# More turns between a triangular solve and its product, and two small stores issued from ScalarE, in a hybrid decoder layer

## The chip, the cores and the metric

The kernel runs on one core of a Trainium2 chip. Its engines are TensorE (PE), VectorE (DVE), ScalarE (ACT), GpSimd (POOL) and SyncE (SP, which only issues transfers here). The metric is the device time of one execution in microseconds. A core has 16 DMA engines; transfers are issued from the queues of SP, ACT and POOL.

## What is computed

One inference step of one decoder layer for a prompt of 512 tokens and for 8 single sample tokens, with the same weights. Cut to what matters:

```python
def layer(x, c, buf_k, buf_v, S0, shift0):
    mod = jax.nn.silu(c) @ w_ada + b_ada
    sh1, sc1, gt1, sh2, sc2, gt2 = jnp.split(mod, 6, axis=-1)
    h = _modulate(_rmsnorm(x, g_norm_mix), sh1, sc1)
    q, k, v, p_rwkv = jnp.split(h @ w_in, ATTN_SPLITS, axis=-1)
    # samples: k_all = the 128 cached rows and the new row; likewise v_all
    att = _banded_attention(q, k_all, v_all, q_pos, k_pos, attn_sinks)
    new_k, new_v = k_all[:, T:], v_all[:, T:]       # the last 128 rows
    rw, S, last_row = _rwkv7_mix(p_rwkv, shift0, S0, ...)
    x = x + gt1[:, None, :] * (jnp.concatenate([att, rw], axis=-1) @ w_out)
    h2 = _modulate(_rmsnorm(x, g_norm_ffn), sh2, sc2)
    gate, up = jnp.split(h2 @ w_ffn_in, 2, axis=-1)
    x = x + gt2[:, None, :] * ((jax.nn.silu(gate) * up) @ w_ffn_out)
    return x, new_k, new_v, S, last_row
# inside _rwkv7_mix, per head, token after token:
#   S_t = S_{t-1} diag(w_t) + (S_{t-1} a_t) b_t^T + v_t k_t^T ;  y_t = S_t r_t
```

Everything is float32. The model has width 2048, 16 query heads and 4 key heads of 64 in the attention half, 16 heads of 64 in the RWKV half.

## The kernel before

**Stages.** The start computes the modulation and the norm. Then comes the RWKV stage, in which the columns of `w_in` are multiplied tile by tile, and the recurrence of the 16 heads runs beside it, two heads (a pair) at a time, eight pairs. Next are the attention beside the first parts of `w_out`, the rest of `w_out`, the first FFN product and the second.

**Products.** A float32 product is made of three float32r products of high and low halves. `unit` loads 128x512 weights from SP's queue (`raw`, three buffers), ScalarE casts the high half (`wh`), VectorE subtracts for the low half (`wl`), and `mm3` issues one *group*: six matmuls of 128x260, the pairs of `wh` and high, `wh` and low, `wl` and high. One unit serves four groups.

**Turns.** After each group the main loop calls `pump`, which gives a turn to each background job that is due. Jobs are Python generators: what one does up to its next `yield` is written into the program at that place. So a bare `yield` in a loop lets more main groups be written ahead of the job's next step. Paced engine wrappers add estimated costs, from which a job's next due time comes. The framework then orders each engine's instructions from what was written, with ready work ahead of waiting work, so one moved step moves its neighbours too. Each engine works through its own order strictly from the front; only its waits are on other engines.

**The solve.** The recurrence is done in chunks of 32 tokens. Per pair, `rwkv_rest` solves 32x32 triangular systems on VectorE (`Tt`, 31 steps of two instructions). The result is written to DRAM (`TTd`, four transfers, two from SP and two from POOL) and read back in another layout (`Td`, from POOL). VectorE copies it into block-diagonal form (`TT`). Then come a number of bare turns, and then for each of the two heads the product `pu` of `L3` and `TT` on PE. After that the chain over the 16 chunks begins (`psc` on PE, `Z` on ScalarE), four small matmuls a turn. The jobs of several pairs are under way at the same time: `rwkv_prep1` and `rwkv_prep2` prepare the next pair (`pw`, `pa`, `pn`, `pG`, `pA`, `pT`, `pg`, `pb`; `lf` are their small weights). `ada_gen` multiplies the rest of the modulation weights (`ada`, weights `ar`). None of them depends on `w_in`'s main tiles except through the buffers.

**The new rows.** At the attention's start `kv_gen` loads keys and values, transposes the values, and `new_kv_sample` transposes the samples' new key and value rows (`KVS`) into `ptx`. VectorE copies them to `kst`, a buffer of the tag `q` (four buffers), and to `VSt`. Two transfers of 8 KB write them to the outputs `ks` and `vs`. The tag `q` is used in turn by the two value loads, `kst`, and the query tiles of `attn_pair`, so the fourth query tile takes `kst`'s place:

```python
q = ap.tile([P, T], F32, tag="q", bufs=4, name=self.nm("q"))
nc.sync.dma_start(q, self.qd[t])
```

Other loads of that time: `x1` (520 KB each) and `s3`, weights of the FFN loaded ahead from SP and added to from POOL (`accum_op`, L1503 and L1504). `attn_decode` computes the samples' attention with the small products `plx` and `psc`. PSUM tiles of `aux` have two buffers, used in turn by all jobs; `plx` takes one that the products `pl` of `attn_pair` held, which VectorE reads with a mask row (`Lg`, `sm`).

Of the kernel before, what the change touches and what calls it, by code (L numbers as in the profile page):

```python
# [63 lines left out]
class Kern:  # L64
# [642 lines left out]
    def rwkv_rest(self, d):  # L707
        nc, I, rc = self.px, self.I, self.rc
        hp, L3, PC = (d[n] for n in ("hp", "L3", "PC"))
# [25 lines left out]
        for c4 in range(4):  # L735
            ro = slice(32 * c4, 32 * c4 + 32)
            nc.vector.tensor_copy(TT[ro, :, 32 * c4:32 * c4 + 32], Td[ro])
        for _ in range(8):
            yield
        for e in range(2):  # L740
            pu = self.aux("pu")
# [143 lines left out]
    def new_kv_sample(self):  # L885
        nc, I, O, ap = self.px, self.I, self.O, self.ap
        pt = self.aux("ptx")
        for i in range(4):
            nc.tensor.transpose(pt[0:8, i * 128:(i + 1) * 128], self.KVS[:, i].rearrange("p h s -> p (h s)"), self.ident)
        kt = ap.tile([8, 256], F32, tag="q", bufs=4, name="kst")  # L890
        self.VSt = ap.tile([8, 256], F32, name="VSt")
        nc.vector.tensor_copy(kt, pt[0:8, 0:256])
        nc.vector.tensor_copy(self.VSt, pt[0:8, 256:512])
        nc.gpsimd.dma_start(O["ks"][:, 127, :], kt)
        nc.gpsimd.dma_start(O["vs"][:, 127, :], self.VSt)

    def attn_pair(self, t, d):
        nc, I, ap = self.px, self.I, self.ap
# [856 lines left out]
```

## Time and profile before

| | |
|---|---|
| median of 3 runs | 2631.68 us (2631.5 to 2631.95) |
| the profiled execution | 2632.03 us, its span 2630.3 us |
| PE busy | 2526.8 us (96%) |
| VectorE busy | 1650.7 us (63%) |
| ScalarE busy | 1167.3 us (44%) |
| POOL busy | 382.3 us (15%) |
| granted PE clock, mean | 0.98 |
| moved by DMA | 460.20 MB, mean 175 GB/s |

A row of the timeline reads: start, duration, engine, line, operation, tile written, tile read, shapes, count; in brackets the idle time of the engine ahead of it and what ended that. Matmuls overlap, so their durations are longer than the time from start to start. A row of the windows reads: stretch, its length, then busy time and count of PE, weight loads, VectorE, ScalarE and POOL, and at the end the granted PE clock, the share of the DMA engines and the GB/s. A row of the waits reads: who waited for whom, total us, times, longest. Instructions issued through the pacing wrapper all have the line L49, so tiles tell them apart. SPq, ACTq and POOLq are transfers being issued.

### The profile page before, as it was taken

The numbers are of one execution on the slowest core, as the hardware profiler recorded it, in microseconds if no ns is written. First come the engines' busy times: TensorE is split into PE (matmuls) and PEld (weight loads), VectorE is DVE, ScalarE is ACT, GpSimd is POOL, SyncE is SP. The second block draws the span as 40 slices with busy tenths as digits, with TensorE's granted clock in tenths as the row PEclk, the third lists the DMA queues.
The fourth block names the chain that finished last, engine by engine and source line by source line (L and its number), as shares of the span: only waits on it lengthen the run. The fifth ranks groups of instructions, "written<-read, shape, count | busy, mean of one in ns | idle before, by whom it ended". The sixth has DMA issues, their size and how long they took to land. (4 is left out here: it accounts for less than half of the span.)

```text
span 2630.3 us, 58954 instructions
## 1 busy us (share of the span) xinstructions
PE 2526.8 (96%) x23373; PEld 2359.7 (90%) x23373; DVE 1650.7 (63%) x3628; ACT 1167.3 (44%) x2413; POOL 382.3 (15%) x529
## 2 busy tenths in 40 slices
PE   7898999999999999998999999999999999999998
PEld 4587878887888988898999999999999999999997
DVE  5566554766656453678777777777777763444456
ACT  3233556566545333557444444444444432222225
POOL 0011111221203010021122122122122000000003
PEclk9998999999999997999999999999999999999999
DMA  9865556655433674246587687688688353443333
GB/s 341 297 202 182 164 172 220 193 189 172 140 111 129 216 224 120 93 156 204 156 228 210 170 218 213 168 214 222 164 214 224 114 181 93 125 126 102 116 105 110
DMA packets 241797, 460.20 MB, mean 175 GB/s; under 512 B 32480, under 2 KB 44656, under 8 KB 241488
## 3 DMA queue, kind: packets, MB, share of 16 engines
q1 hardware_dynamic: 206320, 377.25, 43.8%
q0 software_dynamic: 34560, 78.13, 13.5%
q8 instruction: 183, 3.00, 0.5%
q10 hardware_dynamic: 640, 1.05, 0.2%
q14 instruction: 94, 0.77, 0.1%
HBM read 421.73 MB, written 35.59 MB: 174 GB/s over the span
## 5 line engine op out<-in xcount | busy, mean ns | idle before, releaser
L89 ACT CAST wh<-raw 128x512 fp32r<-128x512 f32 (+2 forms) x410 | 247.4, 606 | 474.2 <-PE pf L99 286.0
L92 DVE TENSOR_TENSOR wl<-raw,wh 128x512 fp32r<-128x512 f32 (+2 forms) x410 | 285.1, 698 | 244.9 <-ACT wh L89 238.5
L99 PE MATMUL pf<-go,wh 128*128 128x260 f32 x2560 | 414.1, 281 | 0.0
L99 PEld LDWEIGHTS pf<-go,wh 128*128 128x128 f32 x2560 | 354.0, 188 | 0.1
L1283 ACT CAST wh<-sr 128x512 fp32r<-128x512 f32 x320 | 197.9, 621 | 258.0 <-PE pm L1454 223.8
L99 PE MATMUL pm<-hH,wh 128*128 128x260 f32 (+1 forms) x1248 | 291.1, 313 | 7.2 <-ACT wh L89 6.4
L1284 DVE TENSOR_TENSOR wl<-sr,wh 128x512 fp32r<-128x512 f32 x320 | 220.2, 688 | 83.1 <-ACT wh L1283 76.0
L99 PE MATMUL pf<-go,wl 128*128 128x260 f32 x1280 | 267.7, 282 | 0.0
L99 PE MATMUL pm<-hH,wl 128*128 128x260 f32 (+1 forms) x1248 | 262.8, 290 | 5.0 <-DVE wl L92 4.9
L1454 PE MATMUL pm<-xT,wh 128*128 128x260 f32 x1408 | 263.1, 286 | 1.1 <-DVE pc L1531 0.6
L99 PE MATMUL pm<-hL,wh 128*128 128x260 f32 (+1 forms) x1248 | 259.3, 289 | 0.0
L1454 PE MATMUL pm<-T,wh 128*128 128x260 f32 x1408 | 257.6, 283 | 0.0
L99 PEld LDWEIGHTS pm<-hH,wh 128*128 128x128 f32 (+1 forms) x1248 | 194.3, 190 | 46.5 <-issue 19.7
L1454 PEld LDWEIGHTS pm<-xT,wh 128*128 128x128 f32 x1408 | 216.8, 188 | 7.7 <-DVE pc L1531 2.8
L1454 PEld LDWEIGHTS pm<-T,wh 128*128 128x128 f32 x1408 | 216.9, 188 | 0.0
L99 PEld LDWEIGHTS pm<-hH,wl 128*128 128x128 f32 (+1 forms) x1248 | 196.4, 191 | 13.8 <-DVE wl L92 8.3
L1454 PE MATMUL pm<-B0H,wl 128*128 128x260 f32 x704 | 200.9, 286 | 7.7 <-DVE wl L1284 7.1
L1454 PE MATMUL pm<-B0H,wh 128*128 128x260 f32 x704 | 200.1, 284 | 2.9 <-DVE acct L1220 1.6
L99 PEld LDWEIGHTS pf<-go,wl 128*128 128x128 f32 x1280 | 201.0, 188 | 0.0
L99 PEld LDWEIGHTS pm<-hL,wh 128*128 128x128 f32 (+1 forms) x1248 | 195.6, 191 | 4.5 <-issue 2.9
L1454 PE MATMUL pm<-T,wl 128*128 128x260 f32 x704 | 198.7, 282 | 0.3 <-DVE wl L1284 0.3
L1454 PE MATMUL pm<-B0L,wh 128*128 128x260 f32 x704 | 198.9, 283 | 0.0
(425 smaller groups left out, 5236.8 us busy)
## 6 DMA issues: line engine op xcount, KB each, us to landing
ar<-in_w_ada SPq DMA_DIRECT2D x256, 256.0 KB, 4.2
sr<-in_w_fi SPq DMA_DIRECT2D x176, 256.0 KB, 4.4
raw<-in_w_fo SPq DMA_DIRECT2D x176, 256.0 KB, 2.6
raw<-in_w_in SPq DMA_DIRECT2D x144, 256.0 KB, 3.9
araw<-in_w_ada SPq DMA_DIRECT2D x64, 512.0 KB, 6.6
raw<-in_w_fi SPq DMA_DIRECT2D x120, 256.0 KB, 4.3
s<-in_w_fi SPq DMA_DIRECT2D x80, 256.0 KB, 5.9
s<-in_w_fi POOLq DMA_DIRECT2D x80, 256.0 KB, 7.2
```

The costliest lines, as they stand in the source:

```text
L89: nc.scalar.copy(wh[:, :n], raw[:, :n])
L92: nc.vector.tensor_tensor(wl[:, :n], raw[:, :n], wh[:, :n].bitcast(F32), ALU.subtract)
L99: nc.tensor.matmul(ps[:m, bank, :HB], w, a[:, k, h, :], start=first and i == 0, stop=last and i == 2, skip_group_check=True,)
L1283: nc.scalar.copy(H, src)
L1284: nc.vector.tensor_tensor(L, src, H.bitcast(F32), ALU.subtract)
L1454: nc.tensor.matmul(ps[:, :HB], x[:, s], y, start=g == k == i == 0, stop=g == 1 and k == 3 and i == 2, skip_group_check=True)
```

## The change

`rwkv_rest` takes 18 bare turns instead of 8 between the copy into `TT` and the product for the first pair (`hp` 0), and 10 instead of 8 for the seven others. `new_kv_sample` issues its two stores from ScalarE's queue instead of POOL's.

```diff
@@ rwkv_rest
         for c4 in range(4):
             ro = slice(32 * c4, 32 * c4 + 32)
             nc.vector.tensor_copy(TT[ro, :, 32 * c4:32 * c4 + 32], Td[ro])
-        for _ in range(8):
+        for _ in range(18 if hp == 0 else 10):
             yield
         for e in range(2):
             pu = self.aux("pu")
@@ new_kv_sample
         nc.vector.tensor_copy(kt, pt[0:8, 0:256])
         nc.vector.tensor_copy(self.VSt, pt[0:8, 256:512])
-        nc.gpsimd.dma_start(O["ks"][:, 127, :], kt)
-        nc.gpsimd.dma_start(O["vs"][:, 127, :], self.VSt)
+        nc.scalar.dma_start(O["ks"][:, 127, :], kt)
+        nc.scalar.dma_start(O["vs"][:, 127, :], self.VSt)
```

In the order of the instructions these places change. The rows are in the order in which the engine takes them; a row reads: line, operation, tile written, tiles read, shape, count. `pm` is the main product of `w_in`, and the numbers tell buffers apart. On PE, ahead of the first pair's first `pu`, before:

```order
L99 MATMUL pm_2994<-hH,wl_2998 128x260 x2
L322 MATMUL ada_2861<-ar_2963,cT 32x128 x4
L322 MATMUL ada_2861<-ar_2964,cT 32x128
L49 MATMUL pu_2983<-TT,L_288_1790 128x128 x4
L322 MATMUL ada_2861<-ar_2964,cT 32x128 x3
```

and after:

```order
L99 MATMUL pm_2988<-hH,wl_3082 128x260 x2
L322 MATMUL ada_2861<-ar_3051,cT 32x128 x4
L322 MATMUL ada_2861<-ar_3052,cT 32x128 x4
L322 MATMUL ada_2861<-ar_3053,cT 32x128 x4
L322 MATMUL ada_2861<-ar_3054,cT 32x128 x4
L49 MATMUL pu_3113<-TT,L_288_1790 128x128 x4
```

The product stands behind later weight units and a later round of `ada`. On VectorE, at the copy into `TT` of the same pair, before:

```order
L92 TENSOR_TENSOR wl_3088<-raw_3085,wh_3087 128x512
L49 SCALAR_TENSOR_TENSOR tF_2657<-pc_2167,par,tF_2657 128x512
L49 COPY TT<-Td_2828 32x8x32 x4
L49 SCALAR_TENSOR_TENSOR tA_2780<-tF_2657,tA_2780 128x512
L92 TENSOR_TENSOR lf_3134<-raw_3135,lf_3134 128x256
```

and after:

```order
L49 SCALAR_TENSOR_TENSOR tF_2657<-pc_2167,par,tF_2657 128x512
L92 TENSOR_TENSOR lf_3124<-raw_3125,lf_3124 128x256
L49 COPY TT<-Td_2828 32x8x32 x4
L49 SCALAR_TENSOR_TENSOR tA_2780<-tF_2657,tA_2780 128x512
L92 TENSOR_TENSOR wl_3082<-raw_3079,wh_3081 128x512
```

The cut of `lf` has moved ahead of the copy, and a cut of a main weight unit follows it. On POOL, at the attention's start:

```order
 L49 DMA out_vp<-Vt 128x256
 L1504 DMA s_2308_16277<-in_w_fi 128x512
-L49 DMA out_ks<-kst 8x256
-L49 DMA out_vs<-VSt 8x256
 L1504 DMA s_2333_16418<-in_w_fi 128x512
 L1504 DMA s_2352_16546<-in_w_fi 128x512
```

The two stores leave POOL's queue; on ScalarE they come between two casts of `w_out` weights. In PE's order nothing is moved from the attention's start on.

## The prediction

> **What bounds the kernel now.** I read the page first, then the chain of waits, PE's list of waits, and the timelines around the two places that the diff touches.
>
> ```profile
> span 2630.3 us, 58954 instructions
> 2116.30 477.88 PE pf L99 x3984
> PE pu L49 <- DVE TT L49: 18.4, 5, 10.1
> PE plx L49 <- DVE sm L49: 5.5, 1, 5.5
> PE po L99 <- ACT wh L89: 3.3, 1, 3.3
> PE ssq L402 <- DVE tC L400: 10.4, 3, 10.0
> ```
>
> The second row is from the chain of waits: at the end PE runs 478 us without a gap, and the chain ahead of it is PE again. So time that PE loses anywhere earlier is lost at the end, one for one. Of PE's waits, the first row of the four is exactly the product `pu` that the change moves; the second is in the attention decode, and it will turn out to hang on the two stores.
>
> **The first pair's product.** PE, then VectorE, POOL and SyncE around it:
>
> ```profile
> 247.69 0.40 PE L99 MATMUL pm<-hH,wh 128*128 128x260 f32 x2
> 247.93 0.40 PE L99 MATMUL pm<-hL,wh 128*128 128x260 f32 x2
> 248.16 0.40 PE L99 MATMUL pm<-hH,wl 128*128 128x260 f32 x2
> 248.49 0.62 PE L322 MATMUL ada<-ar,cT 128*32 128x128 f32 x10
> 259.17 2.04 PE L49 MATMUL pu<-TT,L 128*128 128x128 f32 x8 [10.05 <-DVE TT L49]
> 266.55 1.08 PE L322 MATMUL ada<-ar,cT 128*32 128x128 f32 x32
> 247.87 0.17 DVE L724 TENSOR_TENSOR Tt<-Tt,stmp 128x8 f32<-128x8 f32 x1
> 257.84 1.18 DVE L49 COPY TT<-Td 32x256 f32<-32x256 f32 x4 [4.85 <-DMA Td<-TTd]
> 259.05 0.69 DVE L49 SCALAR_TENSOR_TENSOR tA<-tF,tA 128x512 f32<-128x512 f32 x1
> 251.73 0.92 POOL L732 DMA_DIRECT2D Td<-TTd  x1 [2.21 <-DMA TTd<-Tt]
> 250.20 1.81 SPq L317 DMA_DIRECT2D ar<-in_w_ada  x4
> ```
>
> The solve ends at 248.04, its result goes out to DRAM and back, lands at 257.84, and VectorE has copied it by 259.02. PE was there at 249.11 and waits 10.05 us. The change doesn't shorten that trip; it only puts more PE work ahead of the wait. One turn with work is one group of six matmuls, 3 x 0.24 = 0.72 us from start to start (first three rows). PE before and after, ahead of the first `pu`:
>
> ```order
> L99 MATMUL pm_2994<-hH,wh_2997 128x260 x2
> L99 MATMUL pm_2994<-hL,wh_2997 128x260 x2
> L99 MATMUL pm_2994<-hH,wl_2998 128x260 x2
> L322 MATMUL ada_2861<-ar_2963,cT 32x128 x4
> L322 MATMUL ada_2861<-ar_2964,cT 32x128
> L49 MATMUL pu_2983<-TT,L_288_1790 128x128 x4
> ```
>
> ```order
> L99 MATMUL pm_2988<-hH,wl_3042 128x260 x2
> L99 MATMUL pm_2988<-hH,wh_3081 128x260 x2
> L99 MATMUL pm_2988<-hL,wh_3081 128x260 x2
> L99 MATMUL pm_2988<-hH,wl_3082 128x260 x2
> L99 MATMUL pm_2988<-hH,wh_3081 128x260 x2
> L99 MATMUL pm_2988<-hL,wh_3081 128x260 x2
> L99 MATMUL pm_2988<-hH,wl_3082 128x260 x2
> L322 MATMUL ada_2861<-ar_3051,cT 32x128 x4
> L322 MATMUL ada_2861<-ar_3052,cT 32x128 x4
> L322 MATMUL ada_2861<-ar_3053,cT 32x128 x4
> L322 MATMUL ada_2861<-ar_3054,cT 32x128 x4
> L49 MATMUL pu_3113<-TT,L_288_1790 128x128 x4
> ```
>
> Counted over the whole order, `pu` now comes 9 groups and 27 `ada` matmuls later: 9 x 0.72 = 6.5, and 27/16 x 1.08 = 1.8 (the profile has two records for each `ada` matmul), together 8.3 us. But the third of the weight units now ahead of `pu` (3081, 3082) needs its low half from VectorE, and there it stands behind the copy that waits:
>
> ```order
> L92 TENSOR_TENSOR wl_3042<-raw_3039,wh_3041 128x512
> L49 SCALAR_TENSOR_TENSOR tF_2657<-pc_2167,par,tF_2657 128x512
> L92 TENSOR_TENSOR lf_3124<-raw_3125,lf_3124 128x256
> L49 COPY TT<-Td_2828 32x8x32 x4
> L49 SCALAR_TENSOR_TENSOR tA_2780<-tF_2657,tA_2780 128x512
> L92 TENSOR_TENSOR wl_3082<-raw_3079,wh_3081 128x512
> ```
>
> Before, the two units in front of `pu` were both cut ahead of the copy. So PE will wait again, for `wl` in place of `TT`: the copy ends at 259.02, the row at 259.05 takes 0.69, a cut 0.65, which makes 260.35. Then 0.24 + 0.72 + 1.08 of PE work are left, and `pu` starts at 262.4, 3.2 us later than before with 8.3 us more done. Gain 8.3 - 3.2 = **5.1 us**. The `ada` weights on the way (issued at 250.20) land near 255; that splits the wait in two and leaves its end where it is. What else is new ahead of the copy is the cut of `lf`, whose load takes the place in SyncE's queue that a load of twice its size had; it should land before Td. Bounds: 0 (the copy comes 5 us later) to 8.3.
>
> The pause also costs clock:
>
> ```profile
> 252.00:259.00 7.00, 0.00 (x0) 0.00 (x0) 2.11 (x6) 1.17 (x3) 2.53 (x8) 0.57 0.78 253
> 259.00:262.00 3.00, 2.83 (x24) 2.57 (x27) 2.97 (x7) 0.88 (x2) 0.10 (x1) 0.50 0.16 57
> 262.00:266.00 4.00, 4.00 (x40) 3.62 (x31) 3.00 (x4) 0.65 (x2) 2.28 (x3) 0.84 0.74 260
> 330.00:340.00 10.00, 6.97 (x58) 5.98 (x56) 3.94 (x8) 4.35 (x13) 2.12 (x7) 1.00 0.51 162
> 484.13 1.13 PE L49 MATMUL pu<-TT,L 128*128 128x128 f32 x8 [0.78 <-DVE TT L49]
> 336.63 2.05 PE L49 MATMUL pu<-TT,L 128*128 128x128 f32 x16 [3.03 <-DVE TT L49]
> 623.86 1.13 PE L49 MATMUL pu<-TT,L 128*128 128x128 f32 x8 [3.58 <-DVE TT L49]
> 788.11 2.05 PE L49 MATMUL pu<-TT,L 128*128 128x128 f32 x16 [0.91 <-DVE TT L49]
> 393.26 1.05 PE L49 MATMUL pu<-TT,L 128*128 128x128 f32 x8
> 389.99 1.18 DVE L49 COPY TT<-Td 32x256 f32<-32x256 f32 x4 [4.92 <-DMA Td<-TTd]
> ```
>
> The clock (the number ahead of the last two) is 0.50 when PE restarts; eight `pu` records take 2.04 us against 1.13 at full clock, and until 263 some 2 us are lost. The 3.03 us pause of the second pair left the clock at 1.00. With the pause cut to about half and split I take back **0.5 us** of the 2 (bounds 0 and 2). The Trainium skill (TensorE: Matmul & The Clock Gate, Part 1) says the clock halves after an idle window of about 3.4 us; the two pauses agree, and by it two pauses under 3.4 us would give the whole 2 us back.
>
> **The other pairs.** The rows at 336.63, 484.13, 623.86 and 788.11 hold the rest of the 18.4 us: 3.03 + 0.78 + 3.58 + 0.91 = 8.3. Two more turns are two groups, 1.44 us: they can cover 1.44 + 0.78 + 1.44 + 0.91 = 4.6. But everything after the first pair is interleaved anew. The third pair did not wait (its copy ended at 391.17, `pu` came at 393.26); in the new order only 12 groups stand between its solve and `pu`, where 17 stood: 3.6 us of cover less against 2.1 of slack, and with the smaller matmuls gone from there up to 5.7 us of new wait. I charge 3. Net **1.6 us**, bounds -4 and 8.3.
>
> **The stores.** SyncE, then POOL, ScalarE, VectorE and PE:
>
> ```profile
> SPq L49 <- DMA out_ks<-kst: 11.5, 1, 11.5
> 926.47 13.64 SPq L49 DMA_DIRECT2D q<-qd  x4
> 940.21 7.91 SPq L87 DMA_DIRECT2D raw<-in_w_out  x4
> 928.96 1.27 POOL L49 DMA_DIRECT2D out_ks<-kst  x1
> out_ks<-kst POOLq DMA_DIRECT2D x1, 8.0 KB, 10.8
> RR<-tC ACTq DMA_DIRECT2D x8, 128.0 KB, 2.6
> 928.03 0.62 ACT L89 CAST wh<-raw 128x512 fp32r<-128x512 f32 x1 [2.68 <-PE po L99]
> 946.41 1.23 ACT L89 CAST wh<-raw 128x512 fp32r<-128x512 f32 x2 [11.93 <-DMA raw<-in_w_out]
> 926.47 0.40 DVE L49 COPY VSt<-ptx 8x256 f32<-8x256 f32 x1
> 947.06 0.69 DVE L92 TENSOR_TENSOR wl<-raw,wh 128x512 fp32r<-128x512 f32 x1 [8.60 <-ACT wh L89]
> 948.62 0.21 PE L49 MATMUL plx<-KVS,rstd 64*32 64x1 f32 x1 [5.52 <-DVE sm L49]
> 948.00:951.00 3.00, 2.38 (x63) 2.37 (x63) 2.86 (x13) 1.73 (x5) 0.00 (x0) 0.50 0.35 107
> ```
>
> `kst` is one of four buffers of tag `q`. The fourth `q` load takes it over, so SyncE stands until the store has read it: 11.5 us, for 8 KB that took 10.8 us to land behind POOL's large loads. Behind it in SyncE's queue are the loads of `w_out`; these come at 946.4, the cast, the cut and the mask row behind them follow, and PE's `plx` waits 5.52 us for a PSUM buffer. The change on ScalarE:
>
> ```order
>  L89 CAST wh_12136<-raw_12134 128x512
> +L49 DMA out_ks<-kst 8x256
> +L49 DMA out_vs<-VSt 8x256
>  L89 CAST wh_12188<-raw_12186 128x512
>  L89 CAST wh_12230<-raw_12228 128x512
> ```
>
> The stores now wait on ScalarE for VectorE's copies (done 926.87), and the next cast is due at 928.03, so two issues cost ScalarE nothing; they can be 3 us later before PE's next unit is late. POOL loses two issues of about 1.25 us and has idle time there. The store then lands at 929.5 by the 2.6 us of the other transfers of ScalarE's queue (from buffer to buffer, 128 KB), at 937.7 if it takes 10.8 here too. I take 931 to 933, since the DMA engines are as full as before, and SyncE is free 7 to 9 us sooner. The `w_out` load took 6.2 us (940.2 to 946.4); with the four `q` loads now close in front of it I allow 7 to 8: it lands at 940 to 941. `plx` is due at 942.7 and needs it by about 940.5, so up to 1 us of the 5.52 stays. Gain **4.5 us** plus 1.5 of clock (0.50 from 948 to 951): **6 us**, bounds 0 and 7.4. A rule speaks against it: the Trainium skill (DMA: Bandwidth & Descriptors, Issuing engines are not separate DMA queues) says that transfers run on the same 16 engines whoever issues them, and only issue time is saved. By it the store takes 10.8 us again, SyncE goes on at 937.7, and this term is 2.5; the 2.6 us row of ScalarE's queue, from emptier places, doesn't decide it.
>
> **Sum.** 5.1 + 0.5 + 1.6 + 6 = 13.2 us off the profiled execution's 2632.03, which is 0.35 above the median of the runs: 2618.8 and 2618.5. I say 2619.
>
> **Rivals.**
> - Store alone (16%): the wait for `TT` only changes its name, with `wl` or `lf` late and the third pair giving back the rest. 2632 - 6 = 2626. For it: the order of VectorE above. Against: 8.3 us of work are ahead of `pu`, and the copy's time isn't touched.
> - Solve alone (9%): the store is as slow from ScalarE's queue. 2632 - 7.2 - 2.5 = 2622, or 2625 when the fourth `q` load is held by another load.
> - All of it (14%): every wait for `TT` and `plx` goes, 18.4 + 5.5, less 2.5 that PE cannot cover, with 3.5 of clock: 2607.
> - Slower (5%): the waiting copy holds VectorE, and in the new order later pairs meet what the first meets now, a weight cut behind it. Each microsecond by which Td comes later than the cover then costs PE one. Against that the gains are 13; slower by 0.2% takes 18.5 over seven pairs, 2.7 each: 2638. The orders show such a cut ahead of `pu` at the first pair alone.
> - No change (6%): new waits eat all: 2631.
>
> The forecast itself has 50%, with 2613 to 2624 as its own range. About 0.2% (5.3 us) is what a measurement here can tell. Faster: the forecast, all of it, solve alone and most of store alone: 0.83; same 0.12; slower 0.05. The range for 8 in 10 reaches from near "all of it" to beyond "store alone": 2609 to 2628.
>
> **What the new profile would show.** PE's wait ahead of the first `pu` replaced by one of 1 to 4 us for `wl` L92 near 260 and perhaps one for `ar`; the sum of waits on `TT` under 8 us; SyncE's wait for `out_ks` gone or under 4 us, the 11.93 of the cast with it, and `plx` waiting under 2 us. I'd be wrong if Td lands later than 260, if new waits of the chain (`psc` for `Z`) grow, or if a long half-clock stretch appears.

## The result: slower by 1.1%, and the profile after

The changed kernel takes 2656.4 us (median of 6 runs, 2652.8 to 2666.4) against 2631.1 for the kernel before (6 runs, 2625.0 to 2632.0): ratio 1.0109, 95% interval 1.0089 to 1.0129. Forecast were 2619 us and "faster". The execution that was profiled took 2666.4 us (span 2664.2), 10 us over its median, so of the 34 us between the two profiles only about 25 are typical.

PE's waits after, in the same view as before (who waits for whom: total us, times, longest):

```profile
core 0 of [0], span 2664.2 us
PE pu L49 <- DVE TT L49: 13.9, 5, 4.0
PE psc L49 <- ACT Z L49: 10.5, 13, 2.3
PE pm L99 <- DVE wl L92: 8.2, 11, 1.2
PE ada L322 <- DMA ar<-in_w_ada: 3.8, 3, 1.9
```

The sum of waits hardly changed: `pu` lost 4.5 us of wait, the three others gained 10.5. That does not make 34 us. The next view does: both kernels by stage, RWKV (to the last `w_in` group) and attention (to the first FFN group). The columns are stretch, length, busy time of PE, weight loads, VectorE, ScalarE, POOL, then the granted clock. First before:

```profile
200.00:893.00 693.00, 660.46 (x7849) 575.54 (x7848) 416.75 (x1037) 375.13 (x941) 130.41 (x183) 0.97 0.52 166
893.00:1189.00 296.00, 279.25 (x2298) 254.41 (x2296) 168.22 (x543) 128.68 (x322) 38.00 (x63) 0.94 0.52 160
```

Then after:

```profile
200.00:919.00 719.00, 684.25 (x7824) 594.23 (x7824) 406.72 (x1035) 370.60 (x935) 132.20 (x183) 0.95 0.50 160
919.00:1220.00 301.00, 284.32 (x2303) 258.99 (x2302) 169.05 (x543) 129.09 (x322) 35.98 (x61) 0.92 0.51 157
```

About the same number of PE instructions (7849 and 7824) took 26 us longer in the RWKV stage. PE's idle time grew by 2 us only (693.0 - 660.5 = 32.5, 719.0 - 684.3 = 34.7). PE was *busy* 24 us longer with the same work, at a lower clock (0.95 against 0.97). So the list of waits, on which the prediction was built, is the wrong place to look for this loss.

The timeline of after at the first pair (PE, then VectorE), and behind it PE at pairs 1 to 3 (the pairs are counted from 0):

```profile
250.20 0.43 PE L322 MATMUL ada<-ar,cT 128*32 128x128 f32 x8 [1.86 <-DMA ar<-in_w_ada]
257.43 0.51 PE L99 MATMUL pm<-hH,wl 128*128 128x260 f32 x2 [1.01 <-DVE wl L92]
259.60 1.16 PE L49 MATMUL pu<-TT,L 128*128 128x128 f32 x8
254.87 1.18 DVE L49 COPY TT<-Td 32x256 f32<-32x256 f32 x4 [4.43 <-DMA Td<-TTd]
256.69 0.69 DVE L92 TENSOR_TENSOR wl<-raw,wh 128x512 fp32r<-128x512 f32 x1
```

```profile
330.59 3.78 PE L49 MATMUL pu<-TT,L 128*128 128x128 f32 x16 [3.96 <-DVE TT L49]
387.95 2.05 PE L49 MATMUL pu<-TT,L 128*128 128x128 f32 x8 [3.55 <-DVE TT L49]
512.27 3.76 PE L49 MATMUL pu<-TT,L 128*128 128x128 f32 x16 [3.97 <-DVE TT L49]
```

At the first pair the change did what the prediction said: the wait of 10.05 us is gone, two short ones for `ar` and `wl` stand in its place, and `pu` runs at full speed. But pairs 1 to 3, which had waited 3.03, 0 and 0.78 us, now wait 3.5 to 4.0 each, and the products behind take about twice as long (16 records in 3.8 us; 2.05 at full clock before). Windows of after around two of these pauses:

```profile
325.00:330.60 5.60, 1.64 (x23) 1.18 (x21) 1.19 (x5) 0.62 (x2) 0.00 (x0) 0.92 0.84 293
330.60:336.00 5.40, 5.40 (x27) 4.69 (x28) 0.00 (x0) 1.90 (x4) 0.00 (x0) 0.50 0.00 0
506.00:512.00 6.00, 2.30 (x24) 1.96 (x16) 1.87 (x6) 0.00 (x0) 2.56 (x7) 0.88 0.65 188
512.00:517.00 5.00, 4.73 (x33) 4.48 (x37) 0.81 (x2) 1.17 (x2) 0.00 (x0) 0.50 0.30 105
```

The clock is 0.50 when PE restarts. In the RWKV stage such half-clock time, summed from the granted clock, went from 37.5 to 75.1 us. Half of such time is lost: the 16 `pu` records took 3.8 us in it, 2.05 outside.

The pauses are the smaller part. More half-clock stretches stand where PE did not pause at all. The place is the preparation of a pair: `pG` and `pA`, 64 small matmuls each. Before, at pair 3:

```profile
439.09 0.86 PE L49 MATMUL pG<-KB,tA 64*32 64x64 f32 x64
442.10 2.41 PE L49 MATMUL pA<-tC,KB 64*64 64x32 f32 x64
```

After, at the same pair; the windows behind it are from the next view:

```profile
454.23 0.86 PE L49 MATMUL pG<-KB,tA 64*32 64x64 f32 x64
455.93 2.05 PE L49 MATMUL pA<-tC,KB 64*64 64x32 f32 x32
458.24 2.71 PE L49 MATMUL pA<-tC,KB 64*64 64x32 f32 x32
```

```profile
456.00:459.40 3.40, 3.40 (x54) 3.16 (x54) 0.69 (x1) 0.00 (x0) 0.95 (x1) 0.99 0.76 210
459.40:466.20 6.80, 6.80 (x60) 5.75 (x58) 0.69 (x1) 1.79 (x5) 1.02 (x2) 0.50 0.66 209
```

Before, the two heads' matmuls alternate and overlap, 64 in 2.41 us. After, one head's 32 come first and the other's 32 later, 2.05 + 2.71 us. PE is busy for the whole 3.40 us, and yet the next 6.8 us have half the clock. I call this a *lump*. Whether a pair has one is set by the order: `pG` and `pA` take two PSUM tiles each from the same two buffers, and where no more than about one main group stands between them, its halves are ordered apart. The likely reason, read from the order and not tested, is that `pA`'s second tile is not free in time. Such halves stand at pairs 0, 1 and 7 before, and at 0, 1, 3, 4, 6 and 7 after (pair 2 is mixed).

The stores, in the list of SyncE's waits after, and in the timeline (ScalarE's queue, SyncE, PE):

```profile
SPq L87 <- DMA raw<-in_w_out: 9.2, 2, 8.2
SPq L49 <- DMA out_ks<-kst: 1.9, 1, 1.9
```

```profile
952.59 0.59 ACTq L49 DMA_DIRECT2D out_ks<-kst  x1
952.50 5.82 SPq L49 DMA_DIRECT2D q<-qd  x4
958.41 13.38 SPq L87 DMA_DIRECT2D raw<-in_w_out  x4
972.30 0.21 PE L49 MATMUL plx<-KVS,rstd 64*32 64x1 f32 x1 [3.18 <-DVE sm L49]
```

SyncE's wait for `out_ks` fell from 11.5 to 1.9 us as forecast, but the `w_out` loads behind it now wait 8.2 us for an earlier load to land (from the first of the four rows to the end of the last 7.91 us before, 13.38 now). `plx` still waits 3.18 of its 5.52.

### The profile page after: what moved, and what is told of

Its sections match the earlier page's. It is cut to its first block, busy times and chain, and to the rows that moved or that the text cites. A ratio compares the mean times of both kernels' runs of the same rounds, so it can differ in the third digit from the quotient of the medians.

```text
span 2664.2 us, 58948 instructions
## 1 busy us (share of the span) xinstructions
PE 2555.7 (96%) x23373; PEld 2383.3 (89%) x23373; DVE 1644.5 (62%) x3628; ACT 1163.3 (44%) x2409; POOL 381.8 (14%) x527
## 5 line engine op out<-in xcount | busy, mean ns | idle before, releaser
L99 PEld LDWEIGHTS pm<-hH,wh 128*128 128x128 f32 (+1 forms) x1248 | 196.7, 192 | 46.6 <-issue 18.8
```

The source lines that it names most:

```text
L99: nc.tensor.matmul(ps[:m, bank, :HB], w, a[:, k, h, :], start=first and i == 0, stop=last and i == 2, skip_group_check=True,)
```

## Experiments

Each was timed against the kernel before on the same chip; its median there was 2626.8 us for the first four, 2631.2 and 2627.7 for the next two fours, and 2629.0 for the last two.

**The parts alone.** Stores alone, first pair's turns alone, the others' turns alone, all turns without the stores:

```diff
e1_store:  range(8), stores nc.scalar
e2_first:  range(18 if hp == 0 else 8), stores nc.gpsimd
e3_others: range(8 if hp == 0 else 10), stores nc.gpsimd
e4_solve:  range(18 if hp == 0 else 10), stores nc.gpsimd
```

> Only the two stores go from ScalarE's queue, the turns stay at 8 for all pairs; the order of every other instruction is that of the kernel before. In the trace after, SyncE's wait for out_ks shrank from 11.5 to 1.9 us, but a load of w_out behind it then waits 8.2 us for an earlier load to land, and plx still waits 3.2 us (5.5 before). Theory (the stores are a small gain, the loss is the turns'): 2626 to 2630 us, ratio 0.998 to 1.000. Rival (the stores on ScalarE's queue take part in the loss): over 2635.

> Only the first pair has 18 turns, the others 8, stores as before. Theory (the two more turns of the other pairs make the loss, because pairs 1 to 7 hold the new half-clock stretches): the wait at the first pair goes (10 us shorter wait, some of it back), and the rest is as before: 2620 to 2628. Rival (18 turns at the first pair delay its chain by ten turns, and all that is interleaved behind it comes in another order, so that pauses of 3 to 4 us and the half clock come with it): 2640 to 2660, with new half-clock stretches between 300 and 900 us.

> Only pairs 1 to 7 have 10 turns, the first has 8, stores as before. Theory (these two turns make the loss): 2645 to 2660, the first pair's 10 us wait as before, half-clock stretches between 300 and 900 us as in the changed kernel. Rival (the first pair's 18 turns make it): 2625 to 2635.

> 18 and 10 turns as in the changed kernel, stores from POOL's queue as before. Theory (turns make all the loss, stores are a small gain): 2658 to 2663, some 2 to 5 us over the changed kernel's median of 2656.4. Rival (stores take part in the loss): under 2650.

Measured: e1_store 2630.6 us, ratio 1.001 (0.9996 to 1.0024); e2_first 2660.3, 1.0133 (1.0113 to 1.0154); e3_others 2648.0, 1.0085 (1.0066 to 1.0103); e4_solve 2660.8, 1.0137 (1.0113 to 1.0161).

The stores take no part in the loss. e3_others by itself came out as my theory said, that pairs 1 to 7's two turns made the loss; but the theory missed all the same: the first pair's turns alone cost as much as all turns together, although the wait that they remove is gone, and the two effects don't add. What the two share is not a turn but that everything behind is put in a new order.

e1_store keeps every other instruction in its place. In its timeline (SyncE, PE) the wait of `plx` is 1.69 instead of 5.52 us, and the `w_out` loads again take the time:

```profile
922.55 5.15 SPq L49 DMA_DIRECT2D q<-qd  x4
929.44 13.63 SPq L87 DMA_DIRECT2D raw<-in_w_out  x4
943.58 0.19 PE L49 MATMUL plx<-KVS,rstd 64*32 64x1 f32 x1 [1.69 <-DVE sm L49]
```

So 3.8 us are gained at that place, and the total doesn't show them (the interval is -1.1 to +6.3 us). Where they went is not settled.

**Fewer turns, and the lump by itself.** e5_six is the kernel before with six turns at all pairs. e6_serial exchanges two loops, so that `pA`'s halves never alternate (they did at five pairs, 2 to 6); otherwise only eight VectorE rows (the masks that read `pA`) change places.

```diff
e5_six
-        for _ in range(8):
+        for _ in range(6):
e6_serial, in rwkv_prep2
-        for c in range(16):
-            for e in range(2):
+        for e in range(2):
+            for c in range(16):
```

> 6 turns for all pairs instead of 8, stores as before. In its order pA stands one group behind pG, one head's half after the other, at five pairs (0, 1, 3, 6, 7; and at pair 4, where the two halves still alternate), against three in the kernel before and six in the kernel with 18 and 10. Theory (the time is lost where the small matmuls pG and pA come in one lump, which lowers the clock, and which pairs get such a lump is a matter of the new order, not of the turns): 2636 to 2650, slower although the turns are fewer. Rival (each added turn lengthens the chain of the pairs, so fewer turns are faster or cost only longer waits for TT): 2615 to 2632, or up to 8 x 1.4 = 11 us of more wait for TT in the list of waits if slower.

> The kernel before, with the two loops of pA exchanged, so that the 32 matmuls of one head come before the 32 of the other at all pairs; every other instruction of PE, ScalarE, POOL and SyncE keeps its place. Theory (pA costs twice as much when its halves don't alternate, and the lump then lowers the clock): five pairs change from about 2.0 to 4.0 us, 10 us, and where the clock falls 1.7 to 3.4 more each: 2637 to 2650, with new half-clock stretches behind pA at some of pairs 2 to 6. Rival (pA's form has no weight; the loss is in pauses): 2624 to 2632.

Measured: e5_six 2658.6 us, 1.0098 (1.0081 to 1.0116), outside the theory's range too, but on its side: two turns fewer cost about as much as the whole change (in its trace `pA`'s halves stand apart at six pairs, where I had expected five). e6_serial 2647.1 us, 1.0056 (1.0041 to 1.0072): 16 us for five more lumps, about 3 each. PE in e6_serial at pair 3, the windows there, and the kernel before in the second of them:

```profile
442.95 3.71 PE L49 MATMUL pA<-tC,KB 64*64 64x32 f32 x64
```

```profile
443.00:447.00 4.00, 4.00 (x68) 3.96 (x68) 1.13 (x3) 0.62 (x1) 0.94 (x1) 1.00 0.63 189
447.00:450.00 3.00, 3.00 (x42) 2.44 (x41) 1.08 (x2) 0.00 (x0) 1.01 (x2) 0.51 0.10 25
```

```profile
447.00:450.00 3.00, 3.00 (x27) 2.52 (x26) 0.43 (x1) 2.15 (x7) 1.02 (x2) 1.00 0.43 122
```

The same 64 matmuls take 3.71 us in place of 2.41, without a gap on PE, and the clock falls behind them, where before it stayed at 1.00. Over the stage `pA` costs 31.7 us against 23.8 (from each burst's start to PE's next instruction), half-clock time rises from 37.5 to 44.4; it stands behind three of the five new lumps. In the profiled execution the stage is 9.6 us longer than before, about 2 us a lump. The attention stage, where PE's order is the same, is 5.7 us longer too, with 10 us more of half clock. So a lump costs 2 us by the trace and 3 by the medians, and the difference is not settled.

**The lumps taken away.** Six bare turns ahead of `pA`, in the changed kernel (e7_space) and in the kernel before (e8_bspace):

```diff
         yield
+        for _ in range(6):
+            yield
         mrb = self.mr[64:128].unsqueeze(1).broadcast_to([64, 16, 32])
         pA = [self.aux("pA"), self.aux("pA")]
```

> The changed kernel with six bare turns ahead of pA in rwkv_prep2, all pairs. By its order pA stands six groups or more behind pG at all pairs, and its halves alternate at all. Theory (lumps of pG and pA): pA back to about 2.1 us per pair (some 15 us off), half-clock time of the RWKV stage from 75 to about 40 us (17 us off), less up to 10 us for the later end of the preparation: 2630 to 2645. Rival (the pauses ahead of pu and the longer chain make the loss): 2655 to 2670.

> The kernel before (8 turns, stores from POOL) with six bare turns ahead of pA. Its halves then alternate at all eight pairs instead of five. Theory: three lumps go, 3 x 2.5 us and some 13 us of half clock: 2610 to 2622, if no new wait takes it. Rival (any new order of this tuned stage costs 15 to 30 us, whatever the lumps): 2640 to 2660.

Measured: e7_space 2612.2 us, 0.9929 (0.991 to 0.9948), 44 us below the changed kernel. e8_bspace 2609.6 us, 0.9926 (0.9909 to 0.9944): it beats both kernels. PE in e7_space, pair 3:

```profile
438.20 0.86 PE L49 MATMUL pG<-KB,tA 64*32 64x64 f32 x64
446.11 2.06 PE L49 MATMUL pA<-tC,KB 64*64 64x32 f32 x64
```

`pA` stands 7 us behind `pG` and takes 2.06 us. But the gain is more than the lumps can be worth, and the wait for `TT` shrank as well (18.4 before, 13.9 after); e7_space, then e8_bspace:

```profile
PE pu L49 <- DVE TT L49: 4.7, 5, 2.1
```

```profile
PE pu L49 <- DVE TT L49: 6.2, 3, 3.9
```

**The change's parts without lumps, other turns.** All with the six bare turns ahead of `pA` (ten in e12_space_ten):

```diff
e9_space_first:  range(18 if hp == 0 else 8), stores nc.gpsimd
e10_space_store: range(8), stores nc.scalar
e11_space_six:   range(6), stores nc.gpsimd
e12_space_ten:   range(8), stores nc.gpsimd, ten bare turns ahead of pA
```

> The kernel of e8_bspace (six bare turns ahead of pA, 8 turns, stores from POOL: 2609.6) with 18 turns at the first pair alone. By its order pA's halves alternate at all pairs. Theory (18 turns cost 33 us in e2_first because the new order made lumps; without lumps they cost nothing, and they gain nothing either, since the wait at the first pair that they remove is already short in e8_bspace): 2605 to 2616. Rival (18 turns delay the first pair's chain by ten turns, and that is paid for at the end of the stage): 2620 to 2645.

> The kernel of e8_bspace with the two stores from ScalarE's queue; the order of every other instruction is the same. Theory (SyncE's wait for the stores only turns into a wait for the loads of w_out behind them, as in e1_store): the same as e8_bspace within 4 us, 2606 to 2614. Rival (the stores bring the 4.5 to 6 us that the prediction gave them, once the stage ahead is quiet): 2603 to 2605 or less.

> 6 turns for all pairs, as in e5_six (2658.6), and six bare turns ahead of pA. By its order pA's halves alternate at seven pairs, and at the eighth (pair 2) pA stands 19 groups behind pG. Theory (lumps): 2606 to 2622, 36 us or more below e5_six. Rival (e7_space and e8_bspace were lucky orders, and a new order of this stage mostly costs): 2630 to 2660.

> The kernel of e8_bspace with ten bare turns ahead of pA instead of six; pA's halves alternate at all pairs. Theory (what counts is that pA finds its PSUM buffers free and stands apart from pG): no further gain, 2606 to 2618. Rival (the later end of the preparation is paid for): 2620 to 2635.

Measured: e9_space_first 2633.2 us, 1.0026 (1.0011 to 1.004); e10_space_store 2608.4, 0.9925 (0.9906 to 0.9945); e11_space_six 2615.4, 0.9949 (0.9929 to 0.9969); e12_space_ten 2609.7, 0.9932 (0.9915 to 0.9949).

The table of six turns falls from 2658.6 to 2615.4, so the gain is not that of one lucky order. The stores are worth nothing that can be measured here either. e9_space_first went against the theory. In PE's waits, and in the windows at the stage's end, it shows:

```profile
PE ptx L49 <- DMA vf<-kvd: 10.7, 1, 10.7
PE pt L49 <- DVE RR L49: 10.4, 3, 8.0
```

```profile
878.00:894.00 16.00, 6.18 (x28) 5.84 (x29) 3.61 (x7) 2.48 (x5) 0.44 (x1) 0.57 0.87 293
```

The last pair is done at 875 us, where the main groups also end (875.1; in e8_bspace 850 and 867.5). Nothing is left to run beside its last steps and the attention's first loads, PE works 6 of 16 us and then at half clock. So the chain is later, as the rival said, and here it is paid at the end: in the 40 us behind the last `w_in` group PE idles 16.1 us (8.2 in e8_bspace), and in the RWKV stage 29.6 (21.5). That is 16 of the 24 us between the medians; the rest is not placed. Eighteen turns alone do not bring this: with ten turns for the others (e7_space), the kernel took 2612.2 us.

**One bare turn.** What share do lumps have? One turn moves far less than six. `range(1)` ahead of `pA` in the changed kernel (e13_one) and in the kernel before (e14_bone):

> The changed kernel with one bare turn ahead of pA. By its order pA's halves alternate at pairs 0, 2, 3, 5 and 6 (at 5 alone in the changed kernel), and not at 1, 4 and 7. Theory (the lumps carry most of the loss): four lumps less, each worth 3 us (e6_serial) to 6: 2632 to 2645. Rival (the pauses ahead of pu carry it): 2650 to 2660.

> The kernel before with one bare turn ahead of pA; by its order the halves alternate at all eight pairs, at 1 and 6 for half of the matmuls. Theory: about what six turns gave (2609.6), 2608 to 2622. Rival (the six turns helped by what else they moved): 2624 to 2645.

Measured: e13_one 2631.8 us, 1.0015 (1.0001 to 1.0028); e14_bone 2628.0, 0.9994 (0.9984 to 1.0004). The first bears the theory out, the second the rival. In e14_bone the first pair's lump goes. Windows at that lump and behind it, first of the kernel before (`pA` ends at 214), then of e14_bone (at 209), where the clock stays:

```profile
206.00:212.00 6.00, 6.00 (x128) 5.39 (x128) 2.44 (x8) 0.66 (x2) 1.10 (x1) 1.00 0.81 234
212.00:218.80 6.80, 6.80 (x63) 5.96 (x62) 1.39 (x2) 0.62 (x1) 1.04 (x2) 0.50 0.47 135
```

```profile
210.00:217.00 7.00, 7.00 (x81) 6.48 (x79) 1.46 (x3) 3.02 (x6) 1.03 (x2) 1.00 0.73 224
```

But its order has pauses again further on, with half clock behind them (23.9 us of it behind waits of `pu`; in the kernel before 13.7 behind such waits), and they take it all back. e14_bone's waits of `pu`:

```profile
PE pu L49 <- DVE TT L49: 14.1, 4, 6.6
PE pu L49 <- DVE mod L49: 4.4, 1, 4.4
```

The wait for `TT` alone does not decide it: e12_space_ten has 14.1 us of it too and takes 2609.7 us. There PE's other waits are fewer (idle in all 23.8 us in the RWKV stage, 33.5 in e14_bone), and so is half-clock time (27.3 against 47.8).

**The sum over all runs.** For the RWKV stage of each profiled execution: its length from 200 us to the last `w_in` group, PE's idle time in it, its half-clock time, and the time of `pA`. The remainder is the length less idle, less half of the half-clock time, less `pA`. Each row is one execution; those of the changed kernel, e7_space and e8_bspace were 10 to 12 us above their medians, those of e4_solve and e9_space_first 5 below.

| | length | idle | half clock | `pA` | remainder |
|---|---|---|---|---|---|
| before | 692.6 | 32.5 | 37.5 | 23.8 | 617.5 |
| changed | 719.0 | 34.8 | 75.1 | 32.9 | 613.8 |
| e1_store | 691.6 | 32.2 | 37.5 | 23.2 | 617.5 |
| e2_first | 718.0 | 34.4 | 61.4 | 34.6 | 618.3 |
| e3_others | 707.9 | 36.7 | 64.9 | 27.0 | 611.8 |
| e4_solve | 708.6 | 36.2 | 51.2 | 32.0 | 614.8 |
| e5_six | 721.4 | 38.2 | 71.7 | 30.4 | 616.9 |
| e6_serial | 702.2 | 31.4 | 44.4 | 31.7 | 616.9 |
| e7_space | 674.1 | 24.4 | 23.9 | 15.9 | 621.9 |
| e8_bspace | 667.5 | 21.5 | 30.7 | 15.9 | 614.7 |
| e9_space_first | 675.1 | 29.6 | 23.9 | 15.9 | 617.6 |
| e10_space_store | 663.8 | 23.5 | 13.7 | 15.9 | 617.6 |
| e11_space_six | 669.3 | 18.4 | 27.3 | 17.9 | 619.3 |
| e12_space_ten | 669.4 | 23.8 | 27.3 | 15.9 | 616.0 |
| e13_one | 689.2 | 30.4 | 44.4 | 21.3 | 615.3 |
| e14_bone | 691.4 | 33.5 | 47.8 | 17.6 | 616.4 |

The remainder stays within 612 to 622 while the length runs from 664 to 721. (It is a little too low where `pA` itself runs at half clock.) So three numbers carry nearly all that happened in this stage. Before to changed: idle +2.3, half clock +37.6 / 2 = +18.8, `pA` +9.1, remainder -3.7: +26.4. Put by the cause that stands right ahead of each half-clock stretch in the trace, 40.8 us of the changed kernel's 75.1 follow lumps (13.6 before), 20.4 follow waits for `TT` or `ar` (13.6), the rest other runs of small matmuls. Lumps are then about 13.6 + 9.1, some 20 of the 26 us, and pauses the rest. This split is read from the trace; of the runs, only e6_serial measures lumps by themselves.

## Why the prediction was wrong, step by step

To place the loss in time, I gave each PE instruction the time that its kind usually takes (an estimate, from the kernel before), and compared when two kernels had done the same sum of work. Microseconds behind the kernel before (negative: ahead), at times of the kernel before, good to a few us:

| at | 240 | 260 | 320 | 340 | 400 | 460 | 520 | 600 | 640 | 700 | 760 | 860 |
|---|---|---|---|---|---|---|---|---|---|---|---|---|
| changed | -2 | -13 | -11 | -5 | 5 | 7 | 13 | 21 | 17 | 24 | 29 | 28 |
| e13_one | -10 | -19 | -21 | -15 | -15 | -18 | -12 | -9 | -13 | -11 | -4 | -2 |
| e8_bspace | -6 | -15 | -27 | -22 | -19 | -22 | -21 | -25 | -30 | -28 | -26 | -26 |

- **First pair, 5.1 + 0.5 us: right.** The changed kernel came to this place already ahead, and its solve ended at 245.2, not 248.0; from there to the copy it took as long as before (9.7 and 9.8 us). Counted from the solve's end, `pu` came after 14.5 us where I had 14.4. PE stood for 1.86 + 1.01 us in place of 10.05. Of the clock little came back: `pu` ran at full clock, but 3.4 us from 251.2 on ran at half. From 240 to 320 us the table has a gain of 9.
- **The other pairs, +1.6 us, bounds -4 to 8.3: this step failed.** From 320 to 760 us the changed kernel loses about 40. I wrote that everything after the first pair is interleaved anew, and then priced only one wait in the new order, that of `pu` at pair 2. I did not count what stands around the other small matmuls, though the orders of both kernels were there to compare: lumps at six pairs instead of three. And I let a pause of up to 4 us cost its own length, because the clock was full behind the 3.03 us pause; at 3.55 to 3.97 each also brought 3.4 to 6.8 us of half clock. My own row of 3.58 us (at 623.86) was nearer, and the clock had fallen behind it, to half for 3.4 of the 5 us in this window of the kernel before:

```profile
625.00:630.00 5.00, 5.00 (x28) 4.06 (x29) 2.57 (x4) 4.00 (x10) 2.98 (x2) 0.66 0.01 3
```

- **The stores, 6 us, bounds 0 to 7.4: right in place, not in the total.** The wait for `out_ks` went, the store was fast from ScalarE's queue (issued at 952.6, it let the fourth `q` load go at 958.0, 5.4 us later; I had 4 to 6), `plx` gained 2.3 us (3.8 in e1_store, forecast 4.5). e1_store excludes 6 us: its interval ends at a gain of 1.1. What was wrong is the landing of the first `w_out` load. I had allowed 7 to 8 us from its issue; it took 11.6 (11.8 in e1_store, 6.1 before), so that most of what SyncE gained was waited for again. The rule that I weighed, that transfers share the 16 engines whoever issues them (the Trainium skill, DMA: Bandwidth & Descriptors, Issuing engines are not separate DMA queues), would have had the store as slow as before; SyncE waited 1.9 us for it, not 11.5, so the trace does not bear out the 2.5 us that I drew from it. It does fit what came next: the loads, now close together, took nearly twice as long each. ScalarE's cast behind the first of them still waits 9.47 us (11.93 before):

```profile
970.10 0.62 ACT L89 CAST wh<-raw 128x512 fp32r<-128x512 f32 x1 [9.47 <-DMA raw<-in_w_out]
```

- **The slower rival (5%) had the wrong mechanism.** No weight cut behind a waiting copy cost much: the wait for `wl` grew by 2.9 us. What I had named as proof of error came true in another form: not one long half-clock stretch, but thirteen short ones in the RWKV stage where there were six. The waits of the chain, which I had also named, grew from 6.7 to 10.5 us. Two signs that I had forecast did not come: the waits for `TT` add up to 13.9 us, not under 8, and `plx` waits 3.18, not under 2.

What stays open: where e1_store's 3.8 us went, and why the six bare turns cut PE's idle time as well. In the RWKV stage e8_bspace is 25.1 us shorter than the kernel before: 11.0 of idle time, 7.9 of `pA`, 3.4 of clock, 2.8 of remainder. Lumps explain the second. Of the half clock, 13.7 us stood behind lumps before and none does in e8_bspace, but other stretches grew.

## What to carry to other kernels

Where a list of turns or delays sets the interleaving, an added turn is not a local edit: price it by comparing the whole new order, above all where runs of small matmuls stand and how much full-width work lies between them, not by the one wait that it shortens. When PE is busy 96% and a change moves the time, read busy time and granted clock by stage before the list of waits. A spacing that lets two users of the same PSUM buffers keep apart (here six turns ahead of `pA`, 2609.6 us) came with a gain of 22 us on the kernel before, more than the waits that the change went after.

## What the runs showed of the hardware

- **A busy PE can lose its clock.** In e6_serial 64 matmuls of 64 rows x 64 columns of the array, 32 columns each, kept PE busy for 3.71 us without a gap, and the clock behind them was 0.51. The Trainium skill (TensorE: Matmul & The Clock Gate, Part 1) has the clock halve after an idle window of about 3.4 us; the pauses of 3.55 to 3.97 us agree, but here there was no idle time.
- **What stands ahead of a half clock is little work.** The half-clock stretches last 3.41 us or a multiple of it, so I cut the time into slots of that length. Over six profiled executions (before, the change, e1 to e4, up to 1240 us) I weighed each matmul by its share of the array's rows and columns and by its length. Of 108 slots that fell from full to half clock, three quarters followed a slot with under 27% of the dense main groups' rate, and all of them one under about 41%; of some 1840 that stayed at full clock 99% followed one with more than 25%. Between 27% and 41% most stayed. A third of the 108 (36) followed a slot in which PE was busy throughout. This is what goes together in the traces; that such work brings the half clock, only e6_serial tests.
- **Small matmuls on two row halves of the array overlap.** 64 alternating ones took 2.06 us (e7_space), the same 64 one half after the other 3.71 us.
- **These slots run free of the program.** Within one execution all changes of the clock lie on one grid of 3.41 us, to 0.01 us, and it stands differently in each: 0.42 us past the first instruction in the kernel before, 1.98 in the changed one, 3.15 in e1_store. So one kernel can catch more or fewer half-clock slots from run to run: the attention stage, nearly the same work in all kernels, took 295 to 306 us in these profiles, with 33 to 53 us of half clock. Single runs of one kernel differ by 8 to 18 us (six runs or more), and the longer ones mostly have the lower clock: e13_one's shortest took 2627.2 us at a mean of 0.983, its longest 2644.6 at 0.976.
